# The chunked delta rule of a two-layer mixer block: one chain for four heads and both directions instead of one per pair of heads, with the inverses applied ahead of the steps

## The chip, the cores and the metric

One Trainium2 chip, one core of it, all in float32 (the big products as three products of float32 halves). The metric is the device time of one execution in microseconds (us); the kernel before was run three times.

## The reference

Two layers of a block of four mixers over 1024 latent and 256 context tokens, model width 1024, each mixer 256 wide (4 heads of 64): retention, spatial gating, a short convolution and the gated delta rule. One projection of width 3856 feeds all four, one of width 1024 takes them back. The second layer gives the latent tokens alone.

The delta rule is what the change is about. It runs forward and backward in time (`d`), over context and latent tokens, in chunks of 64 tokens, 20 chunks in all:

```python
    lower = jnp.where(idx[:, None] > idx[None, :],
                      jnp.einsum('nbhid,nbhjd->nbhij', kb, kc) * decay, 0.0)
    rhs = jnp.concatenate([vc * bc, kb * jnp.exp(gc)[..., None]], axis=-1)
    sol = lax.linalg.triangular_solve(lower, rhs, left_side=True, lower=True, unit_diagonal=True)
    uc, wc = sol[..., :dv], sol[..., dv:]
...
    def update(s, ui, wi, kti, cdi):
        v_new = ui - jnp.einsum('bhck,bhkv->bhcv', wi, s)
        return s * cdi + jnp.einsum('bhck,bhcv->bhkv', kti, v_new), v_new
...
    def step(s, inp):
        qi, qdi, ki, di, ui, wi, kti, cdi = inp
        s_new, v_new = update(s, ui, wi, kti, cdi)
        intra = jnp.einsum('bhik,bhjk->bhij', qi, ki) * di
        o = jnp.einsum('bhck,bhkv->bhcv', qdi, s) + jnp.einsum('bhij,bhjv->bhiv', intra, v_new)
        return s_new, o
```

q, k and v come from the projection through a convolution of three taps and SiLU; keys and queries are normalised; the output is normalised by head and multiplied by a SiLU gate.

## The kernel before

Activations lie feature-major (128 features by tokens); a projection (`projs`, L444) multiplies 128x128 weight blocks by up to 512 tokens, three matmuls for each (L455, L456, L457: high by high, low by high, high by low). `raw` weights are loaded by SP's queue, split by ACT (`whi`, L415) and POOL (`wlo`, L416). The output projection is L1346 to L1348, the token-major projections `pt` are L494 to L496.

`run` (L1401) takes the layers one after the other. In each, the delta rule is done by two chains, one per pair of heads `hp`, both directions inside a chain (`delta_chain`, L925):

- preparation: decay matrices `gD`, transposes of keys (`gkT`, L959) and values (`gvT`, L980), the products of keys with keys (`gram`, L1003, 64x64 matmuls in all four quarters of the array), times decay to N (L1013); queries the same way; copies by DRAM that bring the 16x16 diagonal blocks to lanes (`lanes`, L1161);
- inverse (`invert`, L1179): 30 pairs of DVE operations substitute in the diagonal blocks (L1193, L1195, 80 lanes, two groups), then blocks of 32 and 64 are put together by small matmuls (`iq` L1223 and L1261, `ip` L1233 and L1271);
- 20 steps, one chunk of each direction per step, each of three dependent phases of four 64x64 matmuls: keys by state (L1073), the inverse by the result (L1082), keys transposed by that (L1096). Between the phases DVE does L1076 (4 operations of 64x64), L1087 (2) and L1102 (2), ACT copies the values out (L1090), POOL the states (L1105).

`delta_out` (L1109) then makes the outputs feature-major: queries times decay are loaded by DMA (`gqd`, L1131), `oi` (L1137, L1138) multiplies states and values, `head_rows` (L639) sums squares, and `finish_heads` multiplies norm and gate.

Everything else is filler. A generator, `flow`, made by `fillers` (L1389), yields projections, short convolution, spatial gating, retention, and the second pair's q, k and v. The call `beside(pe, wait)` (L505) stands ahead of each piece of the chain and draws steps from the generator until about 1.4 times `wait` us of PE work have been put ahead of it; `drain` draws until a condition holds. Code order sets priority; the scheduler of the tile framework then gives each engine its final order, except inside `manual_schedule`.

```python
        self.lead = min(self.lead, 4.0) + pe - wait * 1.4
        least = 0.6 * pe
        while self.lead < 0 or least > 0:
            us = next(self.flow, None)
```

## Time and profile before

| | |
|---|---|
| median of 3 runs | 1591.65 us (1588.36, 1591.65, 1595.11) |
| profiled execution | 1587.09 us, its span 1585.3 us |
| mean granted TensorE clock | 0.954 |
| busy: PE, DVE, ACT, POOL | 1451.0, 814.6, 503.5, 387.4 us |

The span is the time from the first to the last instruction of the profiled execution; its own time lies 1.8 us over it. A busy time counts the time in which an engine executes instructions other than register, branch, semaphore and DMA-issuing ones. PE takes its instructions in order, so what it waits for stops all that is behind. A granted clock of 1.00 is 2.4 GHz, 0.50 is 1.2 GHz. A record of 64x64 or 32x32 is one of the two passes that a float32 matmul makes, a few records are missing from the trace.

### The profile page before, as it was taken

What the parts mean: (1) busy time and instruction counts of PE and PEld (TensorE: products, weight loads), DVE (VectorE), ACT (ScalarE), POOL (GpSimd) and SP (SyncE); (2) the same over time, 40 slices, a digit from 0 to 9 for tenths busy, and PEclk for the clock granted to TensorE, in tenths of its full rate; (3) what the DMA queues carried; (4) which work ended last, traced back from release to release, by engine and by line L of the source; (5) the groups of instructions that cost most, each with busy time, mean ns of one, the idle gap of its engine ahead of it and who ended that gap; (6) DMA issues with size and microseconds to landing.
All of it is one profiled execution on the core that took longest, in us unless ns stands there. A gap on an engine that the chain in (4) does not pass through costs nothing. (4 is left out here: it accounts for less than half of the span.)

```text
span 1585.3 us, 34893 instructions
## 1 busy us (share of the span) xinstructions
PE 1451.0 (92%) x14636; PEld 1152.0 (73%) x14636; DVE 814.6 (51%) x1863; ACT 503.5 (32%) x1061; POOL 387.4 (24%) x560
## 2 busy tenths in 40 slices
PE   4699999999987889999999999988999697999798
PEld 1587887666865667678999877865678466666798
DVE  0655653454278375543556355823543885654333
ACT  3734213122222222224565443212212221322331
POOL 0422222243030022232222123221321301233330
PEclk9899999999988989999999999989999796999899
DMA  8313532342574211145533135330304542122662
GB/s 280 128 41 79 112 73 73 111 150 93 122 170 96 59 41 32 48 114 163 189 125 115 48 76 118 95 114 25 101 2 120 103 101 51 42 54 85 176 212 74
DMA packets 208839, 158.94 MB, mean 100 GB/s; under 512 B 93542, under 2 KB 181034, under 8 KB 208682
## 3 DMA queue, kind: packets, MB, share of 16 engines
q1 hardware_dynamic: 208682, 156.71, 36.1%
q8 instruction: 115, 1.88, 0.5%
q14 instruction: 42, 0.34, 0.1%
HBM read 123.91 MB, written 32.76 MB: 99 GB/s over the span
## 5 line engine op out<-in xcount | busy, mean ns | idle before, releaser
L416 POOL TENSOR_TENSOR wlo<-raw,whi 128x512 fp32r<-128x512 f32 (+1 forms) x152 | 211.9, 1406 | 613.4 <-ACT whi L415 509.3
L1346 PE MATMUL po<-wo,whi 128*128 128x256 f32 x576 | 162.8, 285 | 1.3 <-ACT wo L415 1.3
L1348 PE MATMUL po<-wo,wlo 128*128 128x256 f32 x576 | 162.8, 283 | 0.8 <-POOL wlo L416 0.8
L1105 POOL COPY gS<-cS 64x64 f32<-64x64 f32 x304 | 88.5, 291 | 305.2 <-DVE cS L1102 265.1
L1347 PE MATMUL po<-wo,whi 128*128 128x256 f32 x576 | 162.8, 283 | 0.2 <-POOL wo L416 0.2
L415 ACT CAST whi<-raw 128x512 fp32r<-128x512 f32 (+1 forms) x152 | 92.8, 619 | 144.7 <-PE pj L456 87.3
L1348 PEld LDWEIGHTS po<-wo,wlo 128*128 128x128 f32 x576 | 110.8, 192 | 1.5 <-POOL wlo L416 1.4
L1346 PEld LDWEIGHTS po<-wo,whi 128*128 128x128 f32 x576 | 110.0, 192 | 2.0 <-ACT wo L415 1.5
L1347 PEld LDWEIGHTS po<-wo,whi 128*128 128x128 f32 x576 | 110.6, 192 | 0.5 <-POOL wo L416 0.4
L1076 DVE SCALAR_TENSOR_TENSOR cy<-cb,vtok,gvt 64x64 f32<-64x64 f32 x304 | 73.5, 280 | 70.6 <-PE cb L1073 69.2
L1090 ACT COPY gx<-cb 64x128 f32<-64x128 f32 x160 | 41.6, 260 | 203.3 <-DVE cw L1087 185.4
L455 PE MATMUL pj<-h10h,whi 128*128 128x512 f32 x200 | 87.4, 437 | 0.0
L455 PE MATMUL pj<-h11h,whi 128*128 128x512 f32 x200 | 85.6, 428 | 0.0
L455 PE MATMUL pj<-h01h,whi 128*128 128x512 f32 x200 | 84.5, 423 | 0.5 <-DVE gN L1013 0.5
L1087 DVE TENSOR_TENSOR cw<-cb,gwt 64x128 f32<-64x128 f32 x152 | 43.9, 289 | 78.0 <-PE cb L1082 76.0
L455 PE MATMUL pj<-h00h,whi 128*128 128x512 f32 x200 | 83.2, 416 | 0.8 <-ACT whi L415 0.7
L457 PE MATMUL pj<-h10h,wlo 128*128 128x512 f32 x200 | 83.5, 418 | 0.3 <-POOL wlo L416 0.3
L456 PE MATMUL pj<-h10l,whi 128*128 128x512 f32 x200 | 83.6, 418 | 0.0
L457 PE MATMUL pj<-h00h,wlo 128*128 128x512 f32 x200 | 81.4, 407 | 0.8 <-POOL wlo L416 0.8
L456 PE MATMUL pj<-h11l,whi 128*128 128x512 f32 x200 | 81.9, 409 | 0.0
L457 PE MATMUL pj<-h11h,wlo 128*128 128x512 f32 x200 | 81.2, 406 | 0.0
L456 PE MATMUL pj<-h01l,whi 128*128 128x512 f32 x200 | 81.2, 406 | 0.0
(361 smaller groups left out, 3456.9 us busy)
## 6 DMA issues: line engine op xcount, KB each, us to landing
raw<-in_w_in SPq DMA_DIRECT2D x120, 256.0 KB
wm<-in_w_mod SPq DMA_DIRECT2D x32, 512.0 KB
x<-in_x SPq DMA_DIRECT2D x16, 512.0 KB
wg<-in_w_mod SPq DMA_DIRECT2D x16, 512.0 KB
raw<-yd SPq DMA_DIRECT2D x32, 256.0 KB
gD<-gc SPq DMA_DIRECT2D x32, 160.0 KB
nd<-gN SPq DMA_DIRECT2D x16, 320.0 KB
xd<-x SPq DMA_DIRECT2D x9, 512.0 KB
```

Of the source, the lines that this page charges most:

```text
L415: self.nc.scalar.copy(hi, raw)
L416: (engine or self.nc.gpsimd).tensor_tensor(lo, raw, hi.bitcast(F32), ALU.subtract)
L455: nc.tensor.matmul(b[:, :n], lhsT=hi[:, kc], rhs=hh[:, kc], start=(kc == 0), stop=False)
L456: nc.tensor.matmul(b[:, :n], lhsT=hi[:, kc], rhs=hl[:, kc], start=False, stop=False)
L457: nc.tensor.matmul(b[:, :n], lhsT=lo[:, kc], rhs=hh[:, kc], start=False, stop=(kc == KC - 1))
L1076: done = V.scalar_tensor_tensor(y[rows(c), half(h)], pk[h][rows(c)], vt[rows(c), 3, d, c // 2, h:h + 1], x[d][:, half(h)], ALU.mult, ALU.add)
L1087: done = V.tensor_tensor(heads(xw[rows(c)]), heads(px[d][rows(c)]), wt[rows(c), d, c // 2].unsqueeze(2).to_broadcast([64, 2, 64]), ALU.mult)
L1090: nc.scalar.copy(value(c)[half(d)], px[d][rows(c)])
L1105: nc.gpsimd.tensor_copy(state(c)[half(d), half(h)], new[half(h), half(d)])
L1346: nc.tensor.matmul(b, lhsT=yh[:, kc], rhs=self.W[0, kc, j], start=kc == 0 and jj == 0, stop=False, skip_group_check=True)
L1347: nc.tensor.matmul(b, lhsT=yh[:, kc], rhs=self.W[1, kc, j], start=False, stop=False, skip_group_check=True)
L1348: held = nc.tensor.matmul(b, lhsT=yl[:, kc], rhs=self.W[0, kc, j], start=False, stop=kc == KC - 1 and jj == 1, skip_group_check=True)
```

## The change

One chain per layer for all four heads. The phases become `delta_keys`, `lanes`, `delta_queries`, `invert`, `delta_values`, `delta_solve`, `delta_steps`, `delta_out`, and the projections of q, k and v are drawn per kind for all heads (`delta_pair`), keys first, queries and values as fillers. The lanes of the substitution are 128 in three groups instead of 80 in two. `delta_solve` is new: it multiplies the inverse by keys times exp(g) (`gw`, to the tile `Ws`) and by values (`gu`, back into `Zs`), so that a step has two phases of eight matmuls: W by state and keys by the difference. The state stays in `Ws`, which the output reads, so nothing is copied out. `delta_out` gives token-major tiles of 128 tokens: states (`oS`) and values (`oX`) are multiplied to separate PSUM tiles and scaled by DVE and POOL, squares are summed along the free dimension, and the result is transposed back (`goT`). The gate goes through DRAM (`delta_gate`). The weights of modulation and gates (L241 and L275 before) are loaded in halves of 512 columns.

The core of the diff (`run`, then the loops of `delta_keys`, `invert`, `delta_solve`, `delta_steps` and `delta_out`); the removed steps are those of `delta_chain` above:

```diff
+            self.gates(l)
+            self.flow = self.delta_pair(l, 1, True)
             self.drain()
             self.flow = self.fillers(l, ctx)
-            for hp in range(2):
-                g = self.delta_chain(l, ctx, hp)
-                self.drain(lambda: self.qkv[1] is not None)
-                self.out[hp] = self.delta_out(l, ctx, hp, *g)
+            self.delta_keys(l)
+            self.lanes()
+            self.delta_queries(l, ctx)
+            self.invert()
+            self.delta_values(l)
+            self.delta_solve(l)
+            self.delta_steps(l)
+            self.delta_out(l, ctx)
             self.later += self.w_out(l)
...
+        for hp, k in enumerate(ks):
+            kt, sq = self.slot("gkt", "G"), self.slot("gks", "G")
+            for t0, m in BLOCKS[True]:
+                self.beside(0.5, 1.5)
+                pt = self.ps("gkT")
+                for i in range(0, m, P):
+                    nc.tensor.transpose(pt[:, i:i + P], k[:, t0 + i:t0 + i + P], self.ident)
+                nc.scalar.copy(kt[:, t0:t0 + m], pt[:, :m])
+                nc.scalar.activation(sq[:, t0:t0 + m], pt[:, :m], AF.Square)
...
+                a = slice(2 * d, 2 * d + 3)
+                tmp = lts[d][:, :3 * i * i].rearrange("p (h c k) -> p h c k", h=3, c=i)
+                V.tensor_tensor(tmp, n5[:, a, j, s].unsqueeze(2).to_broadcast([P, 3, i, i]),
+                                x5[:, a, s, s].rearrange("p h k c -> p h c k"), ALU.mult)
+                done = V.tensor_reduce(x5[:, a, j, s], tmp, AX.X, ALU.add, negate=True)
...
+        for hp in range(2):
+            hs = slice(2 * hp, 2 * hp + 2)
+            kt, vtk = self.slot("gkt", "G"), self.slot("gvt", "G")
+            self.after(nc.sync.dma_start(kt, self.ktd[hp]), self.have_z)
+            self.after(nc.sync.dma_start(vtk, self.vtd[hp]), self.have_z)
+            ke = [self.slot("gke", "G") for _ in range(2)]
+            for d in range(2):
+                V.tensor_tensor(four(ke[d]), four(kt), self.eg[:, :, 4 * d + 2 * hp:4 * d + 2 * hp + 2].unsqueeze(3)
+                                .to_broadcast([P, NT, 2, 64]), ALU.mult)
+                nc.gpsimd.tensor_tensor(self.kw5[d][:, hp], four(kt), self.wt[:, d, :, hs].unsqueeze(3).to_broadcast([P, NT, 2, 64]), ALU.mult)
+            for s0 in range(0, 20, 4):
+                self.beside(0.6, 1.0)
+                pw = self.psf("gw")
+                pv = self.ps("gw")
+                with self.tc.manual_schedule(engines={PE}):
+                    for s in range(s0, s0 + 4):
+                        for d, c in enumerate(self.chunks(s)):
+                            p, t = c % 2, c // 2
+                            o = 64 * (s - s0)
+                            for h in range(2):
+                                nc.tensor.matmul((pw, pv)[p][half(h), o:o + 64], lhsT=four(ke[d])[half(p), t, h],
+                                                 rhs=Zc[half(p), s, 2 * hp + h], start=True, stop=True)
+                for p, pp in enumerate((pw, pv)):
+                    a = slice(0, 4, 3) if p == 0 else slice(1, 3)
+                    nc.scalar.copy(Wq[:, s0 // 2:s0 // 2 + 2, a, hp], pp[:, :256].rearrange("p (m a b) -> p m a b", m=2, a=2))
+                self.beside(0.6, 1.0)
+                pu = self.ps("gu")
+                with self.tc.manual_schedule(engines={PE}):
+                    for s in range(s0, s0 + 4):
+                        for h in range(2):
+                            for d, c in enumerate(self.chunks(s)):
+                                p, t = c % 2, c // 2
+                                o = P * (s - s0) + 64 * h
+                                nc.tensor.matmul(pu[half(p), o:o + 64], lhsT=Zc[half(p), s, 2 * hp + h], rhs=four(vtk)[half(p), t, h],
+                                                 start=True, stop=True)
+                self.have_z = V.tensor_copy(Zc[:, s0:s0 + 4, hs], pu.rearrange("p (s h e) -> p s h e", s=4, h=2))
...
+        for s in range(20):
+            cs = self.chunks(s)
+            o = 256 * (s % 2)
+            if s:
+                self.beside(0.4, 1.0)
+                with self.tc.manual_schedule(engines={PE}):
+                    for q in range(2):
+                        for d, c in enumerate(cs):
+                            for h in range(2):
+                                nc.tensor.matmul(banks[half(c % 2), h, o + 64 * q:o + 64 * q + 64], lhsT=Wd[half(h), s, d, q],
+                                                 rhs=Wd[half(h), s - 1, d, q], start=True, stop=True)
+                done = V.tensor_tensor(X4[:, s], X4[:, s], banks[:, :, o:o + P].rearrange("p h (q e) -> p h q e", q=2), ALU.subtract)
...
+            if s < 19:
+                if s:
+                    V.tensor_tensor(self.Ws[:, 256 * s:256 * s + 256].rearrange("p (d i) -> p d i", d=4),
+                                    self.Ws[:, 256 * s - 256:256 * s].rearrange("p (d i) -> p d i", d=4),
+                                    eg[:, s].rearrange("p d q -> p (d q)").unsqueeze(2).to_broadcast([P, 4, 64]), ALU.mult)
+                self.beside(0.4, 1.0)
+                with self.tc.manual_schedule(engines={PE}):
+                    for q in range(2):
+                        for d, c in enumerate(cs):
+                            for h in range(2):
+                                nc.tensor.matmul(banks[half(h), d, o + P + 64 * q:o + P + 64 * q + 64], lhsT=self.kw5[d][half(c % 2), q, c // 2, h],
+                                                 rhs=Xc[half(c % 2), s, 2 * q + h], start=True, stop=True)
+                new = self.Ws[:, 256 * s:256 * s + 256].rearrange("p (d x) -> p d x", d=2)
+                pb = banks[:, :, o + P:o + 2 * P]
+                if s:
+                    V.tensor_tensor(new, new, pb, ALU.add)
+                else:
+                    V.tensor_copy(new, pb)
...
+            self.beside(1.2, 2.0)
+            pS = self.pc.tile([P, 1024], F32, tag="cc", name=f"oS_{self.uid}_{t}").rearrange("p (h x) -> p h x", h=2)
+            pX = self.ps("oX")
+            with self.tc.manual_schedule(engines={PE}):
+                for hp in range(2):
+                    for d in range(2):
+                        for par in range(2):
+                            c = 2 * t + par
+                            s = step(d, c)
+                            for h in range(2):
+                                x = 128 * d + 64 * hp
+                                nc.tensor.matmul(pS[half(par), h, x:x + 64], lhsT=q[half(h), hp, 64 * (c % 4):64 * (c % 4) + 64],
+                                                 rhs=Wd[half(h), s - 1, d, hp] if s else self.zero[half(h)], start=True, stop=True)
+                for h in range(4):
+                    for d in range(2):
+                        for par in range(2):
+                            nc.tensor.matmul(pX[half(par), 64 * h:64 * h + 64], lhsT=A[d][half(par), t % 2, h],
+                                             rhs=Xc[half(par), step(d, 2 * t + par), h], start=d == 0, stop=d == 1)
...
+                eg = self.eg[:, t, 4 * d:4 * d + 4].rearrange("p (q h) -> p h q", q=2).unsqueeze(3).to_broadcast([P, 2, 2, 64])
+                V.tensor_tensor(y, pS[:, :, P * d:P * d + P].rearrange("p h (q e) -> p h q e", q=2), eg, ALU.mult)
+            V.tensor_tensor(ot, ot, pX[:, :256], ALU.add)
+            nc.gpsimd.tensor_tensor(ot, ot, t1, ALU.add)
```

The order of each engine's instructions follows. First, PE in the steps of layer 0, in the kernel before (`cb` are the PSUM tiles of the chain, `gp` keys, `gZ` the inverse, `pj` the filler projections; a line of "..." leaves out three more of the same kind):

```order
L1073 MATMUL cb_2724<-cS_2748,gp_806 64x64
L1073 MATMUL cb_2725<-cS_2748,gp_806 64x64
...
L455 MATMUL pj_2726<-h01h,whi_2507 128x512
L456 MATMUL pj_2726<-h01l,whi_2507 128x512
L457 MATMUL pj_2726<-h01h,wlo_2508 128x512
...
L1082 MATMUL cb_2724<-cy_2765,gZ_2492 64x64 x2
L1082 MATMUL cb_2725<-cy_2765,gZ_2499 64x64 x2
...
L1096 MATMUL cb_2724<-cw_2786,gkt_1163 64x64 x2
L1096 MATMUL cb_2725<-cw_2786,gkt_1163 64x64 x2
```

and in the changed kernel (`gW` holds W and states, `gZ` the values):

```order
L1299 MATMUL cb_4395<-gW_3687 64x64 x8
L506 MATMUL pj_4408<-h1h,whi_4402 128x512
L507 MATMUL pj_4408<-h1l,whi_4402 128x512
L508 MATMUL pj_4408<-h1h,wlo_4403 128x512
...
L1314 MATMUL cb_4395<-gZ_3071,gkw_3685 64x64 x2
L1314 MATMUL cb_4395<-gZ_3071,gkw_3686 64x64 x2
...
L1299 MATMUL cb_4395<-gW_3687 64x64 x8
```

Three phases per step for two heads have become two per step for four, and six filler matmuls stand between phases as before.

Second, PE at the key transposes of layer 0 (`gkT`, `gp` the keys behind convolution and SiLU), before:

```order
L959 MATMUL gkT_1190<-cst,gp_806 128x128 x4
L455 MATMUL pj_1177<-h00h,whi_1167 128x512
L456 MATMUL pj_1177<-h00l,whi_1167 128x512
L457 MATMUL pj_1177<-h00h,wlo_1168 128x512
...
L959 MATMUL gkT_1203<-cst,gp_806 128x128 x4
...
L959 MATMUL gkT_1217<-cst,gp_806 128x128 x2
```

and in the changed kernel, where the transposes of both pairs stand (`gp_106` and `gp_107`):

```order
L506 MATMUL pj_1112<-h1h,whi_1094 128x512
L995 MATMUL gkT_1125<-base,gp_106_841 128x128 x4
L995 MATMUL gkT_1138<-base,gp_106_841 128x128 x4
L507 MATMUL pj_1112<-h1l,whi_1094 128x512
L508 MATMUL pj_1112<-h1h,wlo_1095 128x512
L995 MATMUL gkT_1152<-base,gp_106_841 128x128 x2
L995 MATMUL gkT_1168<-base,gp_107_842 128x128 x4
L995 MATMUL gkT_1187<-base,gp_107_842 128x128 x4
L995 MATMUL gkT_1201<-base,gp_107_842 128x128 x2
L1040 MATMUL gram_1239<-gp_106_841 64x64
```

Six projection matmuls stood between two groups of transposes; now two stand among all twenty, and the products of keys follow.

Third, DVE in one step of layer 0, before (L613 is a filler's):

```order
L1076 SCALAR_TENSOR_TENSOR cy_2765<-cb_2724,vtok_1018,gvt_1234 64x64
L1076 SCALAR_TENSOR_TENSOR cy_2765<-cb_2725,vtok_1018,gvt_1234 64x64
L1076 SCALAR_TENSOR_TENSOR cy_2765<-cb_2724,vtok_1018,gvt_1234 64x64
L1076 SCALAR_TENSOR_TENSOR cy_2765<-cb_2725,vtok_1018,gvt_1234 64x64
L1087 TENSOR_TENSOR cw_2786<-cb_2724,gwt_1228 64x128
L1087 TENSOR_TENSOR cw_2786<-cb_2725,gwt_1228 64x128
L613 TENSOR_TENSOR su_2060<-su_2060,szz_2061 128x512
L1102 SCALAR_TENSOR_TENSOR cS_2798<-cS_2748,geg_1533,cb_2724 128x64
L1102 SCALAR_TENSOR_TENSOR cS_2798<-cS_2748,geg_1533,cb_2725 128x64
L1076 SCALAR_TENSOR_TENSOR cy_2815<-cb_2724,vtok_1018,gvt_1234 64x64
L1076 SCALAR_TENSOR_TENSOR cy_2815<-cb_2725,vtok_1018,gvt_1234 64x64
```

and in the changed kernel (`base` is the decay):

```order
L287 TENSOR_TENSOR base<-modT_4356,base 128x8 x2
L1301 TENSOR_TENSOR gZ_3071<-gZ_3071,cb_4395 128x2x2x64
L1306 TENSOR_TENSOR gW_3687<-gW_3687,base 128x256
L1319 TENSOR_TENSOR gW_3687<-gW_3687,cb_4395 128x256
L601 TENSOR_TENSOR sz_2966<-pj_4408,sz_2966 128x512
```

Eight operations per step and pair have become three for all heads.

## Rows read from the trace of the kernel before

**Rows 1.** The page: the span, and each engine's busy time.

```profile
span 1585.3 us, 34893 instructions
...
PE 1451.0 (92%) x14636; PEld 1152.0 (73%) x14636; DVE 814.6 (51%) x1863; ACT 503.5 (32%) x1061; POOL 387.4 (24%) x560
```

**Rows 2.** Stretches of the span: length, busy time (and records) of PE to POOL, clock, DMA.

```profile
140.00:276.00 136.00, 134.14 (x1781) 110.11 (x1779) 74.17 (x136) 39.53 (x69) 33.12 (x27) 1.00 0.37 86
276.00:396.00 120.00, 119.41 (x998) 79.61 (x998) 58.29 (x179) 27.24 (x69) 38.13 (x91) 1.00 0.36 116
...
430.00:577.00 147.00, 118.08 (x1770) 91.43 (x1768) 98.11 (x208) 38.17 (x76) 28.97 (x25) 0.87 0.41 96
...
940.00:1086.00 146.00, 136.57 (x1672) 106.09 (x1672) 72.55 (x130) 44.24 (x71) 35.01 (x35) 0.93 0.42 104
...
1226.00:1350.00 124.00, 95.22 (x1560) 72.85 (x1558) 85.61 (x189) 32.37 (x63) 21.71 (x21) 0.82 0.38 82
...
1474.00:1500.00 26.00, 17.69 (x212) 16.66 (x212) 8.36 (x10) 9.17 (x14) 4.68 (x3) 0.74 0.52 133
```

**Rows 3.** Timeline of PE in a step: start, length, instruction group.

```profile
303.06 0.39 PE L456 MATMUL pj<-h01l,whi 128*128 128x512 f32 x1
303.29 0.40 PE L457 MATMUL pj<-h01h,wlo 128*128 128x512 f32 x1
303.61 0.46 PE L1082 MATMUL cb<-cy,gZ 64*64 64x64 f32 x8
...
304.33 0.40 PE L456 MATMUL pj<-h01l,whi 128*128 128x512 f32 x1
```

**Rows 4.** Timeline of PE at a product of keys with keys.

```profile
162.47 1.16 PE L1003 MATMUL gram<-gp 64*64 64x64 f32 x64
163.56 0.50 PE L455 MATMUL pj<-h00h,whi 128*128 128x512 f32 x1
```

**Rows 5.** Timeline of PE in the output of the first chain.

```profile
406.24 0.33 PE L1137 MATMUL oi<-gqd,gS 128*64 128x64 f32 x4
406.36 0.34 PE L1138 MATMUL oi<-gA,gx 128*64 128x64 f32 x4
```

**Rows 6.** Groups by line: convolution tap, SiLU, evacuation; count, busy, mean ns, idle before.

```profile
L532 DVE SCALAR_TENSOR_TENSOR conv<-gp,fv,conv 128x1023 f32<-128x1023 f32 (+1 forms) x22 | 24.3, 1135 | 0.2
...
L900 ACT ACTIVATE gp<-conv 128x1280 f32<-128x1280 f32 (+1 forms) x12 | 14.9, 1238 | 25.9 <-DVE conv L533 25.8
...
L960 ACT COPY gkt<-gkT 128x512 f32<-128x512 f32 (+1 forms) x12 | 6.3, 524 | 7.9 <-PE gkT L959 7.9
```

**Rows 7.** Waits of PE by line: us in total, times, longest.

```profile
PE iq L1223 <- DVE xc L1210: 10.3, 1, 10.3
...
PE iq L1261 <- issue: 6.8, 3, 3.7
PE ip L1233 <- issue: 6.1, 5, 2.4
...
PE iq L1223 <- issue: 4.9, 3, 3.5
...
PE cb L1082 <- DVE cy L1076: 1.4, 5, 0.4
```

**Rows 8.** Groups by line: the two operations of the substitution.

```profile
L1193 DVE TENSOR_TENSOR lt<-nl,xl 80x50 f32<-80x50 f32 (+14 forms) x120 | 59.6, 520 | 4.0 <-DMA nl<-nd 3.0
...
L1195 DVE TENSOR_REDUCE xl<-lt 80x10 f32<-80x50 f32 (+14 forms) x120 | 35.2, 316 | 1.2
```

**Rows 9.** Groups by line: DVE in the steps, and an operation of 128x256.

```profile
L1076 DVE SCALAR_TENSOR_TENSOR cy<-cb,vtok,gvt 64x64 f32<-64x64 f32 x304 | 73.5, 280 | 70.6 <-PE cb L1073 69.2
...
L1087 DVE TENSOR_TENSOR cw<-cb,gwt 64x128 f32<-64x128 f32 x152 | 43.9, 289 | 78.0 <-PE cb L1082 76.0
...
L1102 DVE SCALAR_TENSOR_TENSOR cS<-cS,geg,cb 128x64 f32<-128x64 f32 x144 | 37.5, 278 | 66.9 <-PE cb L1096 58.8 <-ACT gx L1090 3.6 <-ACT wo L415 1.4
...
L731 DVE TENSOR_TENSOR rvd<-rv,cst 128x256 f32<-128x256 f32 x40 | 15.3, 431 | 0.0
```

More of the change, by code (lines that the diff above doesn't have):

```diff
@@ L115, in __init__ @@
         self.loaded = None
+        self.Hs = None
+        self.both = {}
         self.rot = None
@@ L262, in mod, with wmod, quarter @@
         return steps
+    def wmod(self, src=None):
+        w = []
+        for j in range(2 if src is not None else 1):
+            self.uid += 1
+            w.append(self.quarter("wm"))
+            if src is not None:
+                self.after(self.nc.sync.dma_start(w[j], src[:, 512 * j:512 * j + 512]), self.recent)
+        return w
+    def quarter(self, nm):
+        self.uid += 1
+        return self.wp.tile([P, 512], F32, tag=f"q{self.layer}", name=f"{nm}{self.uid}", bufs=6)
     def gate(self, l):
@@ new lines, in gates, with big, delta_pair @@
+        nc.sync.dma_start(self.gcd[0].rearrange("k (t i) -> (k t) i", i=P), gr)
+    def big(self, cols, nm, bufs=1):
+        self.uid += 1
+        return self.gp.tile([P, cols], F32, tag=f"{nm}{self.layer}", name=f"{nm}_{self.uid}", bufs=bufs)
+    def delta_pair(self, l, seg, full, behind=None):
+        nc = self.nc
+        col = lambda hp: (11 + seg) * 256 + hp * P
+        bs = [self.slot("gp%d" % seg, "G") for _ in range(2)]
+        ev = lambda b: (lambda p, t0, m: nc.scalar.copy(b[:, t0:t0 + m], p))
+        yield from self.projs(l, BLOCKS[full], *[(col(hp), ev(bs[hp])) for hp in range(2)])
+        n = T if full else TL
+        for hp, b in enumerate(bs):
@@ new lines, in gram @@
+    def gram(self, k, other, hp, tiles, use):
+        nc = self.nc
+        for tt in ([t for t in tiles if t < 8], [t for t in tiles if t >= 8]):
+            if not tt:
+                continue
+            self.beside(0.16 * len(tt), 3.0)
+            pks = [self.ps("gram") for _ in range(2)]
+            with self.tc.manual_schedule(engines={PE}):
+                for i, t in enumerate(tt):
+                    for par in range(2):
+                        for h, pk in enumerate(pks):
+                            c = t * P + 64 * par
+                            r = slice(64 * h, 64 * h + 64)
+                            nc.tensor.matmul(pk[64 * par:64 * par + 64, 64 * i:64 * i + 64], lhsT=k[r, c:c + 64],
+                                             rhs=other[r, c:c + 64], start=True, stop=True)
+            for h, pk in enumerate(pks):
+                use(pk[:, :64 * len(tt)].rearrange("p (t i) -> p t i", i=64), 2 * hp + h, slice(tt[0], tt[-1] + 1))
@@ L1047, in delta_chain @@
-        Z = self.invert(Ns, nl, xl)
-        S = [self.slot("gS", "G") for _ in range(2)]
-        xs = [self.slot("gx", "G") for _ in range(2)]
-        at = lambda y, c: y[c // 10][:, P * (c % 10):P * (c % 10) + P]
-        state, value = (lambda c: at(S, c)), (lambda c: at(xs, c))
-        chunks = lambda s: ((s + 16) % 20, 19 - s)
-        half = lambda j: slice(64 * j, 64 * j + 64)
-        rows = lambda c: half(c % 2)
-        heads = lambda y: y.rearrange("p (h e) -> p h e", h=2)
-        nc.gpsimd.memset(state(16)[:64], 0.0)
@@ L1107, in delta_chain @@
[L1107 to L1118 removed]
+        self.qd = self.dp.tile([2, P, T], F32, name=f"qd{self.uid}")
@@ new lines, in delta_queries @@
+        self.Ad = self.dp.tile([2, P, NT, 4, 64], F32, name=f"Ad{self.uid}")
+        pq = self.ps("gq2")
+        for hp in range(2):
+            nc.sync.dma_start(self.qd[hp, :, :n], qs[hp][:, :n])
+            q2 = self.slot("gq2", "G")
+            nc.scalar.activation(q2[:, :n], qs[hp][:, :n], AF.Square)
+            for t in range(nt):
+                nc.tensor.matmul(pq[:, 20 * hp + 2 * t:20 * hp + 2 * t + 2], lhsT=q2[:, t * P:t * P + P],
+                                 rhs=cst(C_INDQ, 2), start=True, stop=True)
+            self.gram(self.qkv[1][hp], qs[hp], hp, range(nt), use_a)
@@ L1131, in delta_out @@
-            V.tensor_tensor(qd, qd, q, ALU.mult)
-            self.beside(m / 200, 4.0)
-            pi = self.ps("oi")
-            for c in range(c0, c1):
-                for h in range(2):
-                    o, r = 64 * (c - c0), slice(64 * h, 64 * h + 64)
-                    nc.tensor.matmul(pi[r, o:o + 64], lhsT=state(c)[:, r], rhs=qd[:, h, o:o + 64], start=True, stop=False)
-                    nc.tensor.matmul(pi[r, o:o + 64], lhsT=value(c)[:, r], rhs=A_[:, c % 2, h, (c - c0) // 2], start=False, stop=True)
@@ L1214, in invert @@
+        self.beside(0.0, 42.0)
+        xc, qs = self.big(2 * T, "xc"), self.big(2 * T, "gqs")
+        x4 = xc.rearrange("p (d u i) -> p d u i", d=2, u=40)
+        q4 = qs.rearrange("p (d u i) -> p d u i", d=2, u=40)
+        self.after(nc.gpsimd.memset(qs, 0.0), done)
         quad = [slice(32 * q, 32 * q + 32) for q in range(4)]
         for d in range(2):
+            V.transpose(xc[:, T * d:T * d + T], zc[:, T * d:T * d + T])
+        for d in range(2):
             h = slice(16 * d, 16 * d + 16)
-            for u0 in (0, 10):
-                self.beside(1.6, 2.0)
+            for u0 in (0, 20):
+                self.beside(1.6, 1.5)
@@ L1321, in output @@
             self.new_h(l + 1)
-        late = self.small([P, 512], "hg", 1)[:, :2 * P]
+        late = self.raw([P, 2, P])
         before = None
```

751 lines of the change are left out of this document (362 added, 389 removed).

## The prediction

> **What bounds the kernel now.** First the page's span and busy shares [rows 1]: PE is busy 1451.0 of 1585.3 us, 92%, and no other engine is over 51%. So two things can make the kernel shorter: less occupancy of PE, or less of the 134 us in which it idles. Next the busy time by stretch [rows 2], which tells where those 134 us lie. The first two rows are the preparation and the 20 steps of the first chain: PE is busy 134 of 136 and 119 of 120 us at a clock of 1.00. The reader should see the contrast with rows three and five, the preparations of the second chain of each layer: 118.08 of 147 us, and 95.22 of 124 us. There the projections that fill PE beside the chain had been used up, so 28.9 and 28.8 us are idle, and the granted clock falls to 0.87 and 0.82. The last row, the end of the second layer's delta rule, idles 8.3 of 26 us, and the first preparation of layer 1 idles 9.4 of 146.
>
> Third, the steps. PE is full there, so the recurrence waits for nobody; but each phase costs PE time of its own. In the timeline [rows 3] two projection matmuls of 512 columns start 0.23 us apart. With one phase (8 records, 4 matmuls) and one whole filler matmul between them, the next start that I take is 304.33, after 303.29: 1.04 us for two pitches and the phase, so 1.04 - 0.47 = 0.57 us is the phase. Four matmuls alone would be little of that: 64 gram records (32 matmuls in four quarters of the array) take 1.09 us up to the next start, 34 ns per matmul [rows 4]. So most of a phase is the change between full-array and quarter-array work, and it is paid per phase, not per matmul.
>
> **The change part by part, PE's occupancy.** The steps. Before there are 58 phases in each of 4 chains, 232. A phase costs 0.57 us by the timeline. By the whole stage it is more: the first chain's steps fill the stretch of 120 us [rows 2], and hold by the order 210 matmuls of 512 columns (0.235 each, 49), 117 of 256 (half, 14) and 98 small ones (0.1 us each, an estimate, 10); 47 us are left for 58 phases, 0.80, with the stretch's ends in it. Between the two I take 0.66, of which 0.14 is the four matmuls and 0.52 the change of mode. 232 x 0.66 = 153 us go. What comes is 608 matmuls in 76 phases of eight: 76 x (0.52 + 8 x 0.034) = 61 us. Ahead of them stand the new products of the inverse with keys and values: 20 bursts of 16 in four quarters, 20 x (0.52 + 0.54) = 21, and 20 bursts of 16 whose operand and result lie in the same half, so that only two run together. For such a pair the nearest row is the old output, 4 records in 0.12 us, 58 ns per matmul [rows 5]: 20 x (0.52 + 0.93) = 29. Net -42 us; -30 with phases at 0.57, -59 at 0.80.
>
> The output. Before 288 matmuls in 10 groups: 288 x 0.058 + 10 x 0.52 = 22 us. After 288 in four quarters, 288 in two halves and 18 bursts: 9.8 + 16.7 + 9.4 = 36. Net +14. The 80 head-row matmuls that go and the 72 transposes and query sums that come are of like size; I set them at 0 and keep -5 to +6. The modulation weights arrive in halves, which cuts their matmuls into about 33 more runs; no row shows what one more run costs, so between 0 and a full change of mode, 33 x 0.52 = 17, I take 10. **PE sum: -42 + 14 + 10 = -18**, with ends near -50 and +5.
>
> **The idle time.** With one chain per layer there is no second preparation: the 28.9 + 28.8 us go, and so do the 8.3 behind the last output, since the order puts the transposes of the delta output well ahead of the output projection. That is -66. What is late next: (a) the keys of the second head pair. In the new order the ten transposes of pair two follow those of pair one almost at once (second place in the order section), where six projection matmuls stood between groups. PE, which takes its instructions in order, then waits for convolution, SiLU and evacuation: two taps at 1.14 and about as much for the first one, SiLU 1.24, three evacuations near 1.07 (0.52 and its like for the squares) [rows 6], 7.8 us, twice: +16. Everything behind on PE waits too. (b) the inverse. The wait for DVE before its first block matmuls was 10.3 us in one chain, and "issue", time that PE's own sequencer took, another 6.8 + 6.1 + 4.9 = 17.8 over the four chains [rows 7]. The new chains have as many matmuls in bursts of 80 with about 1.4 us of projections between; I keep most of it, +14. (c) The output has one PSUM buffer and retention stays: +7. **Idle: -66 + 37 = -29**, with ends 0 (every stall comes back) and -58.
>
> On the "issue" term the Trainium skill says otherwise: Runtime: NRT & Kernel Launch, section Instruction fetch mechanics, holds that crossing an instruction block is mostly hidden, a fetch running ahead of the sequencer. By that the 14 would be near 0 and the time about 1516. The trace shows such waits only in the bursts of tiny matmuls, so I keep them.
>
> The substitution runs 30 pairs of DVE operations per chain, now on 128 lanes and three groups instead of two: 520 and 316 ns [rows 8] become at most half as long again, 38 us per chain for 25. In layer 0 the first block matmuls waited for nothing after it, as the stretch is 99% busy, and fillers are drawn beside it; hidden, and if the cover were gone it would cost 13 us a layer, which the upper end holds. DVE's part of a step shrinks from four, two and two operations near 0.28 us [rows 9], 2.3 us, to three of 128x256, for which the nearest row is 0.43 us: 1.3 us for all heads. Six filler matmuls, 1.41 us, stand between phases and cover one such operation. The copies to state and value tiles on POOL and ACT go; both are off the path. SP's new waits (inverse done before keys and values are reloaded, last step before queries are) hold back the weight loads queued behind them, yet weights have hardly been late in the trace and the load has a stage of lead: 0.
>
> **The clock.** In the two second preparations the clock of 0.87 and 0.82 means about 2 x 0.13 x 147 = 38 and 2 x 0.18 x 124 = 45 us at 1.2 GHz instead of 2.4 [rows 2]; PE had idled before each fall. Work done there took twice its time, so at most 19 + 22 = 41 us come back; PE was idle in part of it and the new key stage idles too. I take **-12**, ends 0 and -41.
>
> **Sum.** -18 - 29 - 12 = -59 on the profiled execution's 1587.1 us: 1528. That execution lies 4.6 us under the median of 1591.65, so I say **1530 us**.
>
> **The rivals.** Second, more is hidden than I grant: the key stage is covered, "issue" stays small, full clock throughout. Idle -58, clock -20, PE -25: **1484 us**. For it: the first preparation of layer 0 runs 99% busy. Against: the order leaves nothing between the key transposes.
>
> Third, the idle time only moves: one preparation of double width stalls as much as two did, at the same clock. Only the -18 remains: **1569 us**. For it: layer 1's first preparation idles 9.4 us with fillers left. Against: fillers of both head pairs now lie beside one chain.
>
> Fourth, half-and-half products don't run together: in 608 new matmuls (values by the inverse, and the second term of the output) both halves of the rows write one PSUM bank. Taken one after the other, each costs 58 ns more, 35 us: **1563 us**. The Trainium skill says so: TensorEngine Tiling (Array Packing), section Gotcha 1: PSUM Pressure, different row tiles cannot access one PSUM bank at the same time. The rows decide nothing: the gram's row halves write to different banks.
>
> Fifth, slower. A step's new operation waits on DVE behind work of the fillers, and PE waits with it, since all four heads now hang on one link. If each of 76 phases found a convolution tap of 1.2 us before it, +91: **1619 us**. It decides from (59 + 8) / 76 = 0.9 us per phase on. Against: over the 232 phases of before PE's wait for the first operation of this kind was 1.4 us in all [rows 7], with more operations per phase.
>
> That the change doesn't do what it says I can exclude by the order: the phases are 76, and eight matmuls each.
>
> **How the numbers follow.** Forecast (1505 to 1550) 0.53, second 0.15, third 0.13, fourth 0.08, fifth 0.06; 0.05 for the third with PE's sum at its bad end, which is no change. A measurement of this kernel can tell about 0.5%, 8 us, from no change. Faster: 0.53 + 0.15 + 0.13 + 0.08 = 0.89, taken as 0.88; same 0.05; slower 0.07. The range 1478 to 1585 leaves out the fifth and the better half of the second.
>
> **What would show it.** Right: about 150 fewer quarter-array phases, stretches of steps that are full with 76 waits under 0.2 us, no stretch over 100 us below 85% busy, a mean clock above 0.954, PE busy near 1420 us. The key stage should show a wait of 6 to 9 us per layer for ACT or DVE. Wrong: cb waiting for DVE at each phase (fifth), products of inverse and values pitched at 58 ns per record and not 29 (fourth), or idle time near 130 us again (third).

## The result and the profile after

| | before | after |
|---|---|---|
| median of 4 | 1590.01 us (1582.31 to 1595.11) | 1517.52 us (1513.03 to 1519.97) |
| profiled execution, its span | 1587.09, 1585.3 us | 1518.84, 1517.1 us |
| PE busy; PE idle in the span | 1451.0; 134.3 us | 1403.5; 113.6 us |
| mean granted clock | 0.954 | 0.959 |

The ratio is 0.9545, with a 95% interval of 0.9498 to 0.9591: faster by some 72 us, where some 60 were forecast (1530, range 1478 to 1585). Two executions are left out of the medians below: in the run on the link of the steps the profiled one, 1706.64 us at a mean clock of 0.738, and in the run on the second preparations one of 7294.84 us.

The page of the changed kernel, the span and the busy times, against [rows 1]:

```profile
span 1517.1 us, 36024 instructions
...
PE 1403.5 (93%) x15800; PEld 1155.8 (76%) x15800; DVE 712.5 (47%) x1311; ACT 440.1 (29%) x900; POOL 325.8 (21%) x265
```

Of the 68.2 us that the span lost, 47.5 are busy time of PE and 20.7 idle time. DVE lost 102 us of busy time and POOL 62.

Stretches of the changed kernel, in the columns of [rows 2]: in layer 0 the preparation, the inverse, the steps; in layer 1 the key stage and queries, substitution and inverse, the steps.

```profile
105.00:260.00 155.00, 145.23 (x1053) 120.86 (x1052) 97.88 (x152) 49.25 (x77) 40.23 (x39) 0.94 0.53 120
260.00:345.00 85.00, 73.04 (x2167) 55.58 (x2166) 28.68 (x41) 16.51 (x39) 15.60 (x13) 0.88 0.26 82
...
404.00:487.00 83.00, 81.35 (x1003) 62.49 (x1002) 34.56 (x72) 8.10 (x18) 7.97 (x6) 1.00 0.28 88
...
880.00:1000.00 120.00, 103.86 (x779) 85.52 (x778) 62.99 (x99) 43.02 (x69) 37.58 (x37) 0.90 0.47 106
1000.00:1125.00 125.00, 112.92 (x2317) 85.09 (x2315) 75.75 (x107) 24.26 (x52) 26.74 (x21) 0.93 0.38 101
...
1180.00:1262.00 82.00, 78.03 (x959) 59.20 (x958) 52.02 (x116) 12.84 (x26) 12.42 (x10) 1.00 0.16 46
```

No stretch is left like the two second preparations of [rows 2] (idle 28.9 and 28.8 us). What idles instead is spread: 9.8 and 16.1 us around the keys, 12.0 and 12.1 around the inverse. The steps, 83 and 82 us for all four heads, take less than one chain for two heads did (120).

PE in one step, the view of [rows 3]: start, length, group.

```profile
419.57 0.40 PE L508 MATMUL pj<-h1h,wlo 128*128 128x512 f32 x1
419.89 0.46 PE L1314 MATMUL cb<-gZ,gkw 64*64 64x64 f32 x16
420.29 0.50 PE L506 MATMUL pj<-h1h,whi 128*128 128x512 f32 x1
420.62 0.40 PE L507 MATMUL pj<-h1l,whi 128*128 128x512 f32 x1
```

From 419.57 to 420.62 are 1.05 us for two pitches of 0.235 and the phase: 0.58 us. Eight matmuls cost what the four of [rows 3] did. Those four (the inverse by the result) have operand and result in the same half and use two quarters of the array; the eight use all four. The other two phases of a step before use all four as well, and they were cheaper than the one in [rows 3]. The third phase of the same step, in the kernel before:

```profile
305.27 0.39 PE L457 MATMUL pj<-h01h,wlo 128*128 128x512 f32 x1
305.59 0.34 PE L1096 MATMUL cb<-cw,gkt 64*64 64x64 f32 x8
...
306.20 0.39 PE L456 MATMUL pj<-h01l,whi 128*128 128x512 f32 x1
```

From 305.27 to 306.20 are 0.93 us, 0.46 for this phase. Reckoned in this way, the phases that stand whole between matmuls of 512 columns have medians of 0.47 us for four matmuls in four quarters (47 phases) and 0.58 for four in two quarters (23) in the kernel before, and 0.59 for eight in four quarters (23) in the changed one.

The waits of PE, the view of [rows 7]:

```profile
PE pj L506 <- ACT whi L464: 9.0, 2, 6.6
PE iq L1142 <- issue: 7.7, 6, 3.0
PE gkT L995 <- ACT gp L947: 7.5, 3, 4.5
...
PE pj L508 <- POOL wlo L465: 5.3, 3, 3.8
...
PE pj L506 <- issue: 4.6, 2, 4.1
...
PE ip L1153 <- issue: 4.5, 3, 2.2
PE cb L1314 <- DVE gZ L1301: 3.0, 3, 1.2
```

The first, third and fourth rows are the key stage. "issue" goes on in the inverse, and 4.6 us of it stand on the projections right behind the bursts. The steps wait for DVE three times in the last row and twice more ahead of W by state, 5.3 us in all for 76 phases.

DVE, the groups that answer to [rows 8] and [rows 9]:

```profile
L1111 DVE TENSOR_TENSOR lt<-nl,xl 128x3 f32<-128x3 f32 (+14 forms) x60 | 42.1, 705 | 8.5 <-DMA nl<-nd 7.1
...
L1113 DVE TENSOR_REDUCE xl<-lt 128x3 f32<-128x3 f32 (+14 forms) x60 | 24.3, 410 | 1.5
...
L1301 DVE TENSOR_TENSOR gZ<-gZ,cb 128x256 f32<-128x256 f32 x38 | 15.9, 418 | 37.8 <-PE cb L1299 37.8
```

The substitution takes 705 and 410 ns per operation, 66.4 us in all where it took 94.8; per chain 33 for 24. The three operations of a step (418 ns, 464 for the scaling by decay, 418) are 1.3 us, as reckoned.

### The profile page after: what moved, and what is told of

Same layout as the page of the kernel before. It is cut to its first block, busy times and chain, and to the rows that moved or that the text cites. A ratio compares the mean times of both kernels' runs of the same rounds, so it can differ in the third digit from the quotient of the medians.

```text
span 1517.1 us, 36024 instructions
## 1 busy us (share of the span) xinstructions
PE 1403.5 (93%) x15800; PEld 1155.8 (76%) x15800; DVE 712.5 (47%) x1311; ACT 440.1 (29%) x900; POOL 325.8 (21%) x265
## 5 line engine op out<-in xcount | busy, mean ns | idle before, releaser
L465 POOL TENSOR_TENSOR wlo<-raw,whi 128x512 fp32r<-128x512 f32 (+3 forms) x160 | 218.5, 1380 | 928.7 <-ACT whi L464 815.3
L506 PE MATMUL pj<-h0h,whi 128*128 128x512 f32 (+1 forms) x544 | 215.6, 396 | 18.3 <-ACT whi L464 9.0
L508 PE MATMUL pj<-h0h,wlo 128*128 128x512 f32 (+1 forms) x544 | 209.2, 384 | 4.5 <-POOL wlo L465 4.5
L507 PE MATMUL pj<-h0l,whi 128*128 128x512 f32 (+1 forms) x544 | 208.4, 383 | 0.0
L506 PE MATMUL pj<-h1h,whi 128*128 128x512 f32 (+1 forms) x544 | 207.9, 382 | 0.5 <-issue 0.5
L507 PE MATMUL pj<-h1l,whi 128*128 128x512 f32 (+1 forms) x544 | 203.2, 373 | 2.4 <-issue 2.4
L508 PE MATMUL pj<-h1h,wlo 128*128 128x512 f32 (+1 forms) x544 | 202.5, 372 | 0.8 <-POOL wlo L465 0.8
L506 PEld LDWEIGHTS pj<-h0h,whi 128*128 128x128 f32 x544 | 106.2, 195 | 42.3 <-issue 10.1
L508 PEld LDWEIGHTS pj<-h0h,wlo 128*128 128x128 f32 x544 | 106.4, 196 | 27.7 <-POOL wlo L465 5.7
L507 PEld LDWEIGHTS pj<-h0l,whi 128*128 128x128 f32 x544 | 106.5, 196 | 19.9 <-issue 3.3
```

Of the source, the lines that this page charges most:

```text
L465: (engine or self.nc.gpsimd).tensor_tensor(lo, raw, hi.bitcast(F32), ALU.subtract)
L506: nc.tensor.matmul(b[:, :n], lhsT=hi[kc], rhs=self.h(0, kc, t0, n), start=(kc == 0), stop=False)
L507: nc.tensor.matmul(b[:, :n], lhsT=hi[kc], rhs=self.h(1, kc, t0, n), start=False, stop=False)
L508: self.recent = nc.tensor.matmul(b[:, :n], lhsT=lo[kc], rhs=self.h(0, kc, t0, n), start=False, stop=(kc == KC - 1))
```

## The experiments

Times are medians; the changed kernel is 1517.5. Ratios are to the kernel before on the same chip, 0.9545 (0.9498 to 0.9591) for the changed kernel.

### What a burst costs, and what a matmul in it

Two runs add one full-array matmul to a step phase, one ahead of the eight, one between them (the diff shows the second; in the first the line stands ahead of the loop over `q`); a third doubles the eight.

```diff
+                        if q == 1 and s:
+                            o2 = 256 - o
+                            nc.tensor.matmul(banks[:, 0, o2:o2 + 64], lhsT=self.ident, rhs=self.ident[:, :64], start=True, stop=True)
                         for d, c in enumerate(cs):
```

```diff
-                    for q in range(2):
+                    for q in (0, 1, 0, 1):
```

> The changed kernel with one extra full-array matmul of 64 columns put directly ahead of the eight matmuls of 74 of the 76 step phases (its result is read by nobody). Theory A (PE pays for each change between full-array and quarter-array work, hardly for a matmul): the extra matmul stands on the full-array side of a change that is there anyway, so 74 x about 0.1 us, +4 to +10 us over the changed kernel. Theory B (PE pays by matmuls, a change of mode is free): the same, +4 to +10. This run is the measure for the next one.

> The same extra matmuls, but each between the first four and the last four matmuls of its phase, so that every phase is broken into two bursts. Theory A: each break costs one more pair of mode changes, 74 x 0.4 to 0.5 us, so +30 to +37 us over the run with the matmul ahead. Theory B: within 3 us of the run with the matmul ahead.

> The changed kernel with each of the 608 matmuls of the step phases done twice, 16 instead of 8 in a burst, the number of bursts as it is. Theory A: a burst of 16 records in four quarters takes 0.39 us to the next start, of which 0.15 is the way out; 16 more records are 0.25 us at most, 76 x 0.25 = +12 to +20 us. Theory B: doubling the matmuls doubles the 0.57 us of a phase, +43 us.

Measured: 1526.8 us (ratio 0.9615, 0.9573 to 0.9658), 1549.1 (0.9765, 0.9719 to 0.9812), 1537.7 (0.9677, 0.9632 to 0.9721). Ahead of the phase the matmul costs 9 us, as either theory said. In the middle of a phase it costs 22 us more, 0.30 us for each of 74 breaks. A broken phase, PE's timeline of the second run:

```profile
425.83 0.34 PE L1320 MATMUL cb<-gZ,gkw 64*64 64x64 f32 x8
426.10 0.43 PE L1317 MATMUL cb<-base 128*128 128x64 f32 x2
426.47 0.34 PE L1320 MATMUL cb<-gZ,gkw 64*64 64x64 f32 x8
426.74 0.39 PE L506 MATMUL pj<-h0h,whi 128*128 128x256 f32 x1
```

and an unbroken one with twice the matmuls, of the third:

```profile
425.28 0.69 PE L1299 MATMUL cb<-gW 64*64 64x64 f32 x32
425.90 0.39 PE L540 MATMUL pt<-whi,h0h 128*128 128x256 f32 x1
```

The broken phase takes 0.91 us from its first start to the next filler, 16 records and one full-array matmul; 32 records in one burst take 0.62. So A holds and B falls: a burst costs 0.3 us and more by itself, where I had said 0.4 to 0.5. The third run's 20 us are 608 matmuls at 33 ns: matmuls in a burst aren't free, but cheap. The traces give the price of a burst more finely. Bursts in four quarters that stand whole between full-array matmuls, reckoned like the phases above, cost 0.47, 0.59, 0.82 and 1.28 us with 4, 8, 16 (the third run) and 32 matmuls (keys with keys, in the kernel before). That is 0.35 us for the burst and 0.029 for each matmul in it.

### Fewer bursts with the same matmuls

The weights of the gates and of the modulation of layer 1 come in two halves, and by the order the matmuls on the first half ran alone, as soon as it was there. (The modulation weights of layer 0 come whole, and the edit leaves their order as it is.)

```diff
-            for g in range(4):
+            for g in ((2, 3, 0, 1) if l else range(4)):
...
-            for g in range(4):
+            for g in (2, 3, 0, 1):
```

> The modulation and gate weights come in two halves; the matmuls on the half that is loaded last are put first, so that the four of one block stand together. By the order mod and gate runs fall from 38 to 24 and from 32 to 16, 30 bursts fewer, with the same matmuls. Theory A: 30 x 0.4 to 0.5 us, 12 to 15 us under the changed kernel. Theory B: the same time within 3 us.

Measured: 1504.8 us (0.9469, 0.9433 to 0.9506), 12.7 less, though the two intervals touch. PE is busy 1387.3 us, 16.2 less. The two groups in the changed kernel, and with this edit (line, shapes, count, busy, mean ns, idle):

```profile
L273 PE MATMUL mod<-wm,base 128*32 128x256 f32 x256 | 33.1, 458 | 10.7 <-DMA wm<-in_w_mod 10.7
...
L320 PE MATMUL gate<-wm,base 128*32 128x256 f32 x128 | 21.2, 412 | 0.0
```

```profile
L273 PE MATMUL mod<-wm,base 128*32 128x256 f32 x256 | 24.4, 462 | 10.6 <-ACT junk L374 5.9 <-DMA wm<-in_w_mod 4.7
...
L320 PE MATMUL gate<-wm,base 128*32 128x256 f32 x128 | 11.1, 422 | 0.0
```

33.1 + 21.2 us of busy time become 24.4 + 11.1, near the 25.3 + 11.5 of the same groups in the kernel before, from the order of four matmuls alone. It confirms that the "33 more runs" of the sum cost time, and shows that they needn't be paid.

### The link of the steps

```diff
                 done = V.tensor_tensor(X4[:, s], X4[:, s], banks[...], ALU.subtract)
+                done = V.tensor_copy(X4[:, s], X4[:, s])
...
                     V.tensor_tensor(new, new, pb, ALU.add)
+                    V.tensor_copy(new, new)
```

> The changed kernel with one more DVE operation of 128x256 on each link of the steps: the difference and the new state are copied onto themselves before PE may go on, 74 operations of about 0.42 us. If PE's fillers cover the link with room (six matmuls, 1.41 us, for a link of one operation): within 5 us of the changed kernel, the waits of PE for DVE in the steps stay under 10 us in all. If the link sets the pace of the steps (the slower rival of the prediction): 74 x 0.42, +31 us.

Measured: 1525.0 us (0.9583, 0.9549 to 0.9616), 7.5 over the changed kernel, with intervals that overlap. A copy took DVE 0.33 us in this run's profile, so 74 of them lengthened the links by 24 us. By the medians 7.5 of these came through, more than the 5 expected; by the intervals it is anything from nothing to some 15, and in any case far from 31. What PE waited for in an execution of that length isn't on record. The slower rival of the prediction falls, by this and by the 5.3 us that the changed kernel's steps wait for DVE: the fillers cover most of a link even with one more operation on it.

### Where the idle time of the second preparations came from

In the kernel before, the fillers ahead of the third phase are not drawn in a layer's first chain:

```diff
             if s < 19:
-                self.beside(0.32, 1.0)
+                if hp:
+                    self.beside(0.32, 1.0)
```

> The kernel before, with the fillers ahead of the third phase of each step of a layer's first chain not drawn, so that by the order 16 us more of projections lie beside the second preparation of layer 0 (92 for 76) and 6 us more beside that of layer 1, and 17 and 11 us less beside the first steps. Theory A (the second preparations idle because the fillers have been used up): the idle time of the stretch from the second preparation falls by 10 to 16 us in layer 0 and its granted clock rises, while the first steps begin to wait for DVE, 0.3 to 0.5 us at each of their 58 phases; in sum within 10 us of before. Rival (the preparation waits for its own chain of DVE and DMA wherever fillers are): its idle time stays near 29 us and the stretch gets longer by the 16 us; in sum 10 to 20 us above before.

Measured: 1572.1 us (0.989, 0.9859 to 0.9921), 16 us faster than before. First steps and second preparation of layer 0, in the kernel before, and with the edit:

```profile
276.00:395.00 119.00, 118.41 (x989) 79.16 (x988) 58.29 (x179) 26.46 (x67) 38.12 (x90) 1.00 0.35 115
429.00:577.00 148.00, 119.08 (x1777) 92.23 (x1776) 98.11 (x208) 38.96 (x78) 28.97 (x25) 0.87 0.41 95
```

```profile
279.00:387.00 108.00, 107.72 (x846) 66.39 (x842) 56.14 (x172) 21.36 (x58) 30.43 (x88) 1.00 0.32 103
423.00:571.00 148.00, 131.62 (x1923) 104.89 (x1922) 92.65 (x204) 39.99 (x83) 27.86 (x25) 0.92 0.42 101
```

The second preparation of layer 0 keeps its 148 us and does 12.5 us more of PE work in it, at a clock of 0.92 for 0.87; the first steps become 11 us shorter and stay full. So the idle time was a lack of fillers (A), and the part of A that failed is the price: the first steps had more cover than they needed, and didn't begin to wait, so that the sum fell by more than the 10 us expected at most.

### The key stage

The part of `delta_keys` that makes the decay matrices becomes a method of its own, called earlier:

```diff
             self.gates(l)
+            self.delta_decay(l)
             self.flow = self.delta_pair(l, 1, True)
```

> The decay matrices are prepared between the gates and the key projections instead of behind them, so that less of POOL's and DVE's work stands ahead of the weight casts in the key stage. The key stage of the changed kernel waits 6.3 us (layer 0) and 14.9 us (layer 1). If POOL's order there sets the waits for weights: 3 to 6 us under the changed kernel. If the waits are set by ACT and by the chain of convolution, SiLU and evacuation: within 2 us of it.

Measured: 1507.6 us (0.9492, 0.9462 to 0.9521), 9.9 less, though the intervals of the two kernels still touch. Waits of PE:

```profile
PE gkT L1002 <- ACT gp L947: 9.6, 4, 3.6
...
PE pj L508 <- POOL wlo L465: 3.2, 4, 1.3
...
PE pj L506 <- ACT whi L464: 1.7, 2, 1.1
```

The waits for ACT's weight casts fell from 9.0 to 1.7 us, those for POOL's from 5.3 to 3.2; the waits for SiLU grew from 7.5 to 9.6. All of the gain in the key stage is in layer 1, whose waits there fell from 14.9 to 7.0 us; those of layer 0 went from 6.9 to 7.5, SiLU for weights. So in layer 1 the weights were late behind the decay matrices, by more than I had thought, and the chain of convolution and SiLU is what stays.

### A gain that didn't come

```diff
-            for t in range(nt):
-                nc.tensor.matmul(pq[:, 20 * hp + 2 * t:20 * hp + 2 * t + 2], lhsT=q2[:, t * P:t * P + P], rhs=cst(C_INDQ, 2), ...)
+            for t0, m in BLOCKS[ctx]:
+                nc.tensor.matmul(pq[:2, :m], lhsT=cst(C_INDQ, 2), rhs=q2[:, t0:t0 + m], start=True, stop=True)
```

> The changed kernel with its 36 query-sum matmuls (128x128 weights for two columns each, 10 us of PE and a stretch at half clock in each layer) replaced by 10 matmuls of up to 512 columns that give the sums by rows, which a DMA by DRAM brings to token order. Theory A (work with few columns is dear on PE, in its own time and in the granted clock behind it): 10 matmuls at about 0.5 us are 5 us for 10, and the half-clock stretches near 180 and 986 us of the span, worth 3 to 5 us together, go: 6 to 10 us under the changed kernel. Rival: the stretch at half clock comes from something else there and the 4-byte DMA gets in the way of weight loads: 0 to -5 us, the half-clock stretch stays.

> The order of the halves, the query sums by rows and the decay first together. If their gains add: 12.7 us measured for the first, 6 to 10 for the second, 0 to 6 for the third, so 1489 to 1499 us. If what one frees becomes a wait of another stage: above 1500 us.

> As the run with three edits (1502.6 us), but the DMA that brings the query sums to token order in elements of 4 bytes is issued behind the last step instead of in the query stage. If that DMA in its old place held up what lies behind it (PE waited 8.9 us there): 7 to 10 us under the run with three edits, 1492 to 1496 us. If the waits of the inverse for 'issue' (13.2 us there, 5.7 without the edit) are the cost: within 3 us of 1502.

Measured: 1526.7 us (0.9619, 0.9589 to 0.9649) alone, 9 us slower than the changed kernel (the intervals just touch), a miss; 1502.6 (0.9453, 0.9426 to 0.9479) with the two good edits; 1504.5 (0.946, 0.9436 to 0.9484) with the DMA issued late, so that it wasn't the DMA's place. Waits of PE in the first of the three:

```profile
PE ip L1156 <- issue: 12.1, 7, 2.8
...
PE pj L506 <- DVE xl L1116: 7.8, 1, 7.8
```

7.8 us are a projection in layer 1 that waits for DVE while that is in the substitution, and "issue" in the inverse's `ip` rose from 4.5 to 12.1. But the 7.0 us of "issue" on the projections behind the bursts went: all of PE's waits for "issue" together are 24.1 us for 22.9, and in the two versions with the good edits they are 24.2 us with the query sums by rows and 27.0 without. So "issue" isn't what makes the edit slower, though 1504.5 us is what the last expectation said for that cause. Why the new order of the scheduler is worse stays open.

> The order of the halves and the decay first, without the query sums by rows. If their gains add: 12.7 and 9.9 us under the changed kernel's 1517.5, so 1492 to 1498 us. If the second edit's gain was chance of the order: above 1502 us.

Without it: **1493.9 us** (0.9397, 0.9374 to 0.9421). The order of the halves and the decay first add up (12.7 + 9.9 reckoned, 23.6 measured), and this version beats both kernels.

### The inverse's tiny matmuls

```diff
-                    for u in range(20):
+                    for u in [u for u in range(20) for _ in range(2)]:
```

> The changed kernel with the matmuls of the inverse's first level (16 columns) done twice, bursts of 160 instead of 80. Theory A (the waits for 'issue' come from PE's sequencer running short of instructions where they are tiny): the 640 more matmuls cost 1280 records at 7 to 10 ns, about 11 us, and the waits for 'issue' in and behind these bursts, about 17 us in the changed kernel, grow by half to as much again, 8 to 17 us: +19 to +28 us. Rival (fetching is hidden, the waits belong to the place): the records alone, +9 to +14 us, waits within 3 us of 17.

Measured: 1591.0 us (1.0022, 0.9995 to 1.0049), 73 us more, the whole gain of the change. Waits of PE, and the stretches of the inverse:

```profile
PE iq L1142 <- issue: 23.4, 12, 3.2
PE ip L1153 <- issue: 19.0, 11, 2.7
```

```profile
255.00:360.00 105.00, 82.95 (x3194) 68.90 (x3193) 21.88 (x30) 11.79 (x25) 9.96 (x10) 0.67 0.11 34
1045.00:1150.00 105.00, 81.56 (x2423) 67.34 (x2422) 45.88 (x59) 13.81 (x23) 16.65 (x14) 0.74 0.25 61
```

The second row ends within the inverse of layer 1. The waits for "issue" in these bursts go from 12.2 to 42.4 us; as those behind the bursts shrink, all of PE's waits for "issue" go from 22.9 to 46.7. The clock falls to 0.67 and 0.74 in these stretches and from 0.959 to 0.933 in the mean, and PE's busy time rises by 51 us, though the records alone, 2,560 more (the expectation counted half of them) at 10 ns, would be 26. A is right in kind and far too small.

The traces show what PE waits for. Their DMA packets include a queue that the profile calls "instruction"; its packets, MB and share of 16 engines in the changed kernel, and in this run:

```profile
q8 instruction: 124, 2.03, 0.5%
```

```profile
q8 instruction: 144, 2.36, 0.6%
```

20 more packets for 5,120 more instructions (each matmul record has a weight load beside it) are 256 for each packet, of 16 KB. Of the waits for "issue" over 0.15 us, 15 of 18 in the changed kernel and 27 of 29 here end 1.15 to 1.65 us after such a packet has landed, all of those in and behind the inverse's bursts among them; of PE's waits for anything else 2 of 54 and 2 of 50 do. The first burst here:

```profile
263.82 0.65 PE L1142 MATMUL iq<-xc,gN 32*32 32x16 f32 x55
266.39 1.90 PE L1142 MATMUL iq<-xc,gN 32*32 32x16 f32 x128 [1.92 <-issue]
269.84 0.72 PE L1142 MATMUL iq<-xc,gN 32*32 32x16 f32 x36 [1.55 <-issue]
```

From one wait to the next PE runs 128 records, which with their weight loads are the 256 instructions of one packet. Two packets of this queue start 3.3 us apart at the least in either trace, 26 ns for each of 128 records, and a record of 16 columns takes some 10. So the rival falls: PE waits for its instructions.

## Why the prediction was right

The direction and the size held, and so did the main causes: fewer changes between full-array and quarter-array work, and no second preparations that idle. The terms themselves were off, against each other, so that a part of the sum's fit is luck.

**PE's occupancy** was put at -18 us (-50 to +5) and is at least -36: busy time fell by 47.5, of which the clock can have given 11 at most. Three numbers failed in "a phase at 0.66". First, its 0.52 for the change of mode is the phase of [rows 3] less four matmuls at the pitch of four quarters. That phase uses two quarters, where a matmul takes 58 ns, so only 0.35 us are the change, as the bursts of all lengths say. The new phase, put at 0.52 + 8 x 0.034 = 0.80 us, takes 0.59: 76 x 0.21 = 16 us too dear. Second, two of three old phases take 0.47 where they are whole, and all 232 would come to some 117 us instead of 153. Third, "232 phases" was too few bursts: the trace of the kernel before has some 350 runs of step matmuls, as other work breaks its phases some 120 times, against 82 runs now. At the 0.30 us of the second experiment that is some 36 us more, which brings the old steps back to the 153 of the sum: there two errors cancelled. The products ahead of the steps were put at 1.06 and 1.45 us a burst; whole ones take 0.82 and 1.28, 8 us less for all forty. A burst of values, from 373.95 to 375.70 less two pitches:

```profile
373.95 0.40 PE L508 MATMUL pj<-h0h,wlo 128*128 128x512 f32 x1
374.28 1.15 PE L1269 MATMUL gu<-gvt,gZ 64*64 64x64 f32 x32
375.36 0.50 PE L506 MATMUL pj<-h1h,whi 128*128 128x512 f32 x1
375.70 0.39 PE L507 MATMUL pj<-h1l,whi 128*128 128x512 f32 x1
```

It also settles the fourth rival: 1.28 us less 0.35 for the burst are 58 ns for each of 16 matmuls, as for two that run together [rows 5], and not twice that. Of the Trainium skill's rule on row tiles and one PSUM bank (TensorEngine Tiling (Array Packing), Gotcha 1: PSUM Pressure) no cost is seen here. The halves of the modulation weights cost 16 to 18 us against the 10 in the sum.

**Idle time** was put at -29 and is -20.7. What was said to go went. The key stage was put at +16 and waits 21.8 us (1.80, 1.27, 2.42, 0.68 and 0.77 in layer 0; 4.47, 6.57 and 3.85 in layer 1). Two thirds of that is weights that were cast late, which the prediction had set to 0 ("weights have hardly been late"): it thought of the loads, and in layer 1 the decay matrices stood ahead of the casts. The inverse was put at +14 and has 20.4 us of "issue", counting what stands behind its bursts. But the kernel before had 20.0 (the 17.8 of the prediction and 2.2 in `ip`, L1271), of which only the 9.3 in the second preparations are in the -66. So the sum counted the other 10.7 twice: its own 14 would have been some 3 more than what stayed, and 10 more came. On this term the Trainium skill (Runtime: NRT & Kernel Launch, Instruction fetch mechanics) had the waits mostly hidden; the trace disagrees, and the doubled inverse shows PE waiting for packets of instructions.

**The clock** was put at -12. The time at half clock fell from 2 x 0.046 x 1585 = 146 us to 2 x 0.041 x 1517 = 124, worth at most 11. The inverse (0.88) and the key stage (0.90) keep what the second preparations lost.

The second rival's cover didn't come in the key stage and the inverse; of the third's 66 us of stalls some 45 came; the fifth's link was covered. In what was to be seen: 76 phases, steps at 98 and 95% busy and the mean clock above 0.954 were right. Five of the 76 waits are over the 0.2 us named, the longest 1.7. From 844 to 944 us PE is 82.6% busy, below the 85 named, and in the first 100 us 73.9 (66.7 in the kernel before). PE busy near 1420 was 16 too high, and the key stage's 6 to 9 us held in layer 0 alone.

## What to carry to other kernels

Where a dependent chain of small matmuls runs beside full-array work, count its bursts in the final order, not the matmuls or the phases of the code: a burst between full-array matmuls costs 0.35 us here, and each matmul in it 0.03 in four quarters of the array and 0.06 in two. Do what doesn't depend on the recurrence ahead of it, and let the chain be as wide as the array allows. Then look at what starves beside it: a stretch that idles for lack of fillers can be fed from a stretch that has more than it needs, and the pieces of one block belong in the order in which their last operand comes.

## What the hardware showed unasked

Bursts of matmuls of 16 columns cost far more than their records: 2,560 more of them made the kernel 73 us slower, 51 us of it busy time of PE, where the records at 10 ns are 26 and the rest goes with a mean clock of 0.933 for 0.959, and 21 idle time. PE idles in these bursts because its instructions come in packets of 256, at least 3.3 us apart, and at 10 ns a record a burst uses one up in 1.3. The query sums of layer 0, with two columns each, are followed by 10 us at a clock of 0.50 to 0.52 although PE hardly idled ahead of them; with sums by rows that stretch ran at 1.00, while layer 1 fell to half clock at another place near by, where PE had idled for 7.8 us.
